# Ordering a mixture's experts by token count on the chip: places of 128 and of 64 tokens take turns in the expert stage

## The chip, the cores and the metric

One core of a Trainium2 chip runs the whole program once; the metric is the device time of that one launch in microseconds (us). TensorE (PE) multiplies, VectorE (DVE) and ScalarE (ACT) work elementwise, GpSimd (POOL) makes masks and constants, SyncE (SP) issues nearly all loads, and 16 DMA engines carry them.

## The reference, cut to what matters

Two residual layers over x, 256 tokens of 1024 channels, float32. Layer 0 is attention beside a short convolution, then a dense SwiGLU; layer 1 is a recurrent block, then a mixture of 8 experts, each token going to two. The mixture is what the change touches:

```
logits = xf @ w_router                      # [256, 8]
top_logits, top_idx = lax.top_k(logits, 2)
gates = softmax(top_logits)
for each expert e, for its tokens xb:
    hb = silu(xb @ w_gate[e]) * (xb @ w_up[e])   # 1024 -> 3584
    yb = hb @ w_down[e]                          # 3584 -> 1024
out[token] += gate * yb
```

On the inputs that are timed, the reference's router gives the experts 0 to 7, in this order, 67, 78, 65, 56, 63, 63, 62 and 58 tokens.

## The kernel before, in words

All weights are float32 and are read once, from one array laid out in the order of use, in loads of 128 x 2048 elements (1 MB) into a ring of tiles. SP issues them in order; each waits until the ring's tile is free. Each half of a load, a *piece* of 128 x 1024, is split into a high and a low part of fewer bits: ScalarE copies the high part (`hl_of`, L242), VectorE subtracts it from the piece (L243). TensorE then makes three products for every pair of a stationary and a moving tile (`mm3`, L221 to 224): high by high, high by low, low by high.

The expert stage (`experts`, L845) takes the experts 0 to 7 in turn, 128 tokens each. For every expert the hidden width is cut into 7 blocks f of 512. A block has 12 pieces: four each of the gate and the up projection (`g`, `u`) and four of the down projection (`d`) of the block before. The tokens are the stationary side, [channel, 128 tokens]; the weights move through, 512 columns at a time. So a piece is 2 x 3 products of 512 columns, whatever the number of tokens that the expert really has.

What surrounds the products:

- `choices` (L786) ranks every token within its expert. `choose` (L899) makes a 0/1 matrix [token, slot] for two experts at a time, and `gather` (L906) multiplies the normed tokens by it, both parts, in products of 256 columns (two experts of 128 slots).
- After the gate's last piece ScalarE takes its SiLU from PSUM (L998); after the up projection's, VectorE multiplies (L1002). Two pieces later (`TURN`), `turn` (L959) transposes the hidden block on TensorE (four transposes, L962) and splits it (L242, L243).
- `factors` and `back` prepare norm factors and the way back; `out_parts` and `combine` (L967, L976) bring an expert's rows back into the residual in products of 256 columns.
- `gates` (L820) comes at the down projection of block 3, and counts the fullest expert. If an expert has more than 128 tokens, a second pass over all experts runs (L1060 to 1063).

Order of the work: the stage is written out by hand (`manual_schedule`, L1024). After the products of piece n come what they set off (`follow`, L992), what is due at n (`at`), and then the splits of pieces up to n + 5 (`AHEAD`, the number of tile pairs for split pieces; L1055). Each engine works through its own instructions in this order. The ring has 9 tiles, and 2 more from the earlier layers' buffers; in the first round 2 halves besides (`source`, L871).

```
for n in range(len(pieces)):
    products(n)
    ...
    follow(n)
    for fn, a in later.pop(n, ()):
        fn(*a)
    while ready < min(n + 1 + (AHEAD if n < len(pieces) - END else ENDA), ...):
        prepare(ready)
        ready += 1
```

Of the kernel before, what the change touches and what calls it, by code (L numbers as in the profile page):

```python
# [9 lines left out]
F32 = mybir.dt.float32  # L10
# [15 lines left out]
NE = 8  # L26
# [17 lines left out]
# Products that keep the tensor engine's clock up: at the start, and on both sides of the ranks.  # L44
# [13 lines left out]
TURN = 2  # L58
# The ring with the tiles that the first rounds of the experts' weights use besides.
# [16 lines left out]
def _chunks():  # L76
    """The weights in the order in which they are used: name and elements per partition."""
# [12 lines left out]
    prev = []  # L90
    for e in range(NE):
        for f in range(NF):
            c += [(f"m{m}{e}_{f}_{i}", 2048) for m in "gu" for i in range(2)]
            c += prev
            prev = [(f"md{e}_{f}_{i}", 2048) for i in range(2)]
    return c + prev
# [8 lines left out]
NW = _o  # L105


def body(ctx, tc, x_d, w_d, prm_d, bv_d, rt_d, out_d):
# [8 lines left out]
    t2 = ctx.enter_context(tc.tile_pool(name="t2", bufs=5))  # L117
# [33 lines left out]
    def warm(n):  # L151
        """Keeps the clock of the tensor engine up where it would else wait long."""
        p = pz()
        for _ in range(n):
            T.matmul(p[:, 0:P], onesb, onesb, start=True, stop=True)

    def weave(chain, filler):
        """Emits a step of the one, a step of the other, and so on."""
        live = [chain, filler]
        while live:  # L160
            for g in list(live):
                if next(g, live) is live:
                    live.remove(g)
# [4 lines left out]
    # ---- inputs and constants  # L168
# [33 lines left out]
    def halves(k):  # L202
        """A load into two of the tiles of half the size."""
# [22 lines left out]
    def rsqrt(ss, n, inv):  # L226
        """(ss * inv + eps) ** -0.5 by Newton's steps."""
# [12 lines left out]
    def hl_of(src, oh, ol):  # L240
        """src as the sum of two parts of fewer bits."""
# [3 lines left out]
    def scaled(gk):  # L245
        """The residual by the norm's gain, in two parts; the norm's other factor comes later."""
# [9 lines left out]
    def norm_factor(spread=True):  # L256
        """1 / rms of every token: one a partition [128, 2], and along the free dimension [128, 256]."""
# [44 lines left out]
            # Two sums share a bank: only the bank's first product clears it.  # L302
# [31 lines left out]
    def wide_steps(src, hT, o, n):  # L334
        """o[:, j, :] (two of them in a bank) = columns j of the load, [n / 128, 8, 128], by hT."""
# [12 lines left out]
    # ---- layer 0: attention and short convolution  # L348
# [7 lines left out]
    # The distance, and where there is none to be seen, a number that the softmax doesn't survive.  # L356
# [31 lines left out]
    def attention():  # L388
# [36 lines left out]
        # The first block's eight heads see one block of keys, the second's, four at a time, two.  # L425
# [113 lines left out]
    # -8 * softplus(-lambda), its logarithm as a series in t / (2 + t).  # L539
# [20 lines left out]
    # ---- layer 0: SwiGLU  # L560
# [27 lines left out]
    # ---- layer 1: recurrent block  # L588
# [566 lines left out]
```

## Time and profile before

| | |
|---|---|
| time, median of 3 runs | 1446.46 us (1446.17 to 1446.46) |
| span of the profiled execution, first to last instruction | 1447.3 us |
| busy in it: PE, DVE, ACT, POOL | 98%, 83%, 71%, 0% |
| read from HBM | 424.77 MB, 294 GB/s over the span |
| loads of the expert stage | 336 of 1 MB |

The profiled execution is one of its own, beside the timed runs; its span is its time, 0.8 us above their median. The stages, from the stretches of the profile: layer 0 and the recurrent block until about 450 us, the experts from there to the end. A busy engine in these views is one that has an instruction under way; matmuls overlap, so the start-to-start distance of equal instructions is the better price.

### The profile page before, as it was taken

How to read it: one execution, taken by the hardware profiler on the slowest of the kernel's cores; microseconds unless marked ns; L12 is line 12 of the kernel's file. 1: busy time of each engine (PE TensorE's matmuls, PEld its weight loads, DVE VectorE, ACT ScalarE, POOL GpSimd, SP SyncE). 2: the span in 40 equal slices, each digit the busy share in tenths (PEclk: the TensorE clock that was granted, in tenths of full speed). 3: DMA queues.
4: the chain of work that ended last, by engine and by line, in shares of the span. 5: the costliest groups of instructions: out<-in, count | busy, mean ns of one | idle time of the engine just before them, and what ended most of it. 6: DMA issues, size and time to landing. Idle time of an engine off the chain costs nothing.

```text
span 1447.3 us, 20977 instructions
## 1 busy us (share of the span) xinstructions
PE 1422.2 (98%) x8083; PEld 1241.0 (86%) x8083; DVE 1198.5 (83%) x1365; ACT 1025.4 (71%) x1195; POOL 3.0 (0%) x15
## 2 busy tenths in 40 slices
PE   8999999999999999999999999999999999999997
PEld 7799999999988888888888888888888888888886
DVE  6667555556887999988999998899999889999986
ACT  6445444444796888788788778878887887887874
POOL 0000000000000000000000000000000000000000
PEclk9999999999999999999999999999999999999999
DMA  9434455553447899999999989999999999999980
GB/s 374 181 118 174 175 185 194 175 177 144 175 146 287 316 350 383 347 351 360 342 374 375 367 339 365 352 344 377 374 359 351 352 353 348 376 376 343 377 318 32
DMA packets 61451, 427.25 MB, mean 295 GB/s; under 512 B 7200, under 2 KB 7200, under 8 KB 11296
## 3 DMA queue, kind: packets, MB, share of 16 engines
q1 hardware_dynamic: 60624, 425.22, 77.5%
q8 instruction: 65, 1.06, 0.3%
q10 hardware_dynamic: 720, 0.62, 0.1%
q14 instruction: 42, 0.34, 0.1%
HBM read 424.77 MB, written 1.05 MB: 294 GB/s over the span
## 4 chain that ended last, share of the span: by engine, by line
PE 85%; DVE 6%; ACT 4%; DMA 3%; issue 1%; SPq 0%; ACTq 0%
PE pw L222 17%; PE pw L223 17%; PE pw L224 17%; PE pa L222 7%; PE pa L224 7%; PE pa L223 7%; DVE L L243 4%; PE pa L304 3%; PE pa L303 3%; PE pa L305 3%; DMA w<-in_w_dram 2%; PE pz L962 1%; ACT H L217 1%; PE pz L913 1%; ACT H L242 1%
## 5 line engine op out<-in xcount | busy, mean ns | idle before, releaser
L243 DVE TENSOR_TENSOR L<-w,H 128x1024 fp32r<-128x1024 f32 x545 | 647.1, 1218 | 70.0 <-ACT H L242 50.3
L242 ACT ACTIVATE H<-w 128x1024 fp32r<-128x1024 f32 x545 | 563.6, 1056 | 90.7 <-PE pw L224 56.5
L222 PE MATMUL pw<-H,b 128*128 128x512 f32 x896 | 350.3, 391 | 0.7 <-ACT b L914 0.7
L223 PE MATMUL pw<-L,b 128*128 128x512 f32 x896 | 349.1, 390 | 0.0
L224 PE MATMUL pw<-H,b 128*128 128x512 f32 x896 | 348.8, 389 | 0.0
L217 ACT ACTIVATE H<-w 128x1024 fp32r<-128x1024 f32 (+1 forms) x138 | 143.1, 1046 | 169.4 <-PE pw L223 101.5
L218 DVE TENSOR_TENSOR L<-w,H 128x1024 fp32r<-128x1024 f32 (+1 forms) x138 | 165.8, 1207 | 92.2 <-ACT H L217 92.1
L224 PEld LDWEIGHTS pw<-H,b 128*128 128x128 f32 x896 | 168.2, 188 | 35.9 <-ACT b L914 0.6
L222 PEld LDWEIGHTS pw<-H,b 128*128 128x128 f32 x896 | 168.4, 188 | 34.5 <-ACT b L914 1.4
L223 PEld LDWEIGHTS pw<-L,b 128*128 128x128 f32 x896 | 168.4, 188 | 33.0
L222 PE MATMUL pa<-H,b 128*128 128x512 f32 x480 | 192.1, 402 | 4.3 <-ACT H L217 4.3
L222 PE MATMUL pw<-b,H 128*128 128x256 f32 x672 | 191.4, 285 | 2.7 <-DVE b L608 1.4
L224 PE MATMUL pw<-b,L 128*128 128x256 f32 x672 | 191.2, 284 | 0.1
L223 PE MATMUL pw<-b,H 128*128 128x256 f32 x672 | 190.9, 285 | 0.0
L224 PE MATMUL pa<-H,b 128*128 128x512 f32 x480 | 186.9, 389 | 0.0
L223 PE MATMUL pa<-L,b 128*128 128x512 f32 x480 | 186.8, 389 | 0.0
L243 DVE TENSOR_TENSOR L<-b,H 128x1024 fp32r<-128x1024 f32 x128 | 152.8, 1220 | 17.8 <-ACT H L242 14.1
L242 ACT ACTIVATE H<-b 128x1024 fp32r<-128x1024 f32 x128 | 132.7, 1057 | 18.7 <-PE pw L224 11.1
L222 PEld LDWEIGHTS pw<-b,H 128*128 128x128 f32 x672 | 129.4, 193 | 3.8 <-issue 3.7
L224 PEld LDWEIGHTS pw<-b,L 128*128 128x128 f32 x672 | 129.5, 193 | 0.3 <-DVE L L218 0.3
L223 PEld LDWEIGHTS pw<-b,H 128*128 128x128 f32 x672 | 129.4, 193 | 0.2
L222 PEld LDWEIGHTS pa<-H,b 128*128 128x128 f32 x480 | 90.8, 190 | 20.6 <-ACT H L217 4.5
(209 smaller groups left out, 1456.7 us busy)
## 6 DMA issues: line engine op xcount, KB each, us to landing
w<-in_w_dram SPq DMA_DIRECT2D x331, 1024.0 KB, 5.1
b<-in_w_dram SPq DMA_DIRECT2D x60, 1024.0 KB, 5.1
w<-in_w_dram SPq DMA_DIRECT2D x12, 512.0 KB, 6.8
b<-in_w_dram SPq DMA_DIRECT2D x8, 512.0 KB, 6.7
w<-in_w_dram SPq DMA_DIRECT2D x4, 768.0 KB, 7.9
x_sb<-in_x_dram SPq DMA_DIRECT2D x4, 256.0 KB, 7.6
out_dram<-x_sb SPq DMA_DIRECT2D x2, 256.0 KB, 3.1
out_dram<-x_sb ACTq DMA_DIRECT2D x2, 256.0 KB, 3.1
```

The lines of the kernel that those rows point to most:

```text
L217: A.activation(h[:, :n], src, AF.Copy)
L218: V.tensor_sub(l[:, :n], src, h[:, :n].bitcast(F32))
L222: T.matmul(o, a[0], b[0], start=first, stop=False)
L223: T.matmul(o, a[0], b[1], start=False, stop=False)
L224: T.matmul(o, a[1], b[0], start=False, stop=last)
L242: A.activation(oh, src, AF.Copy)
L243: V.tensor_sub(ol, src, oh.bitcast(F32))
L303: T.matmul(o, h[:, c], m[0][:, ks[i], :], start=f and d % 2 == 0, stop=False, skip_group_check=True)
L304: T.matmul(o, h[:, c], m[1][:, ks[i], :], start=False, stop=False, skip_group_check=True)
L305: T.matmul(o, l[:, c], m[0][:, ks[i], :], start=False, stop=z and d % 2 == 1, skip_group_check=True)
L913: T.matmul(p[:, k * S:(k + 1) * S], src[:, t, d:d + P], sel[q][t], start=t == 0, stop=t == 1)
L962: T.transpose(p[:, k * P:(k + 1) * P], sg[:, k * P:(k + 1) * P], ident)
```

## The change

Experts no longer run in the order of their number. After the choices the kernel counts the tokens of every expert and orders the experts by count on the chip; expert 0 always comes first in the order, so that its weights can be loaded before the order is known. Places 0, 2, 4, 6 (`HEAVY`) hold 128 tokens and take the first four experts of the order, places 1, 3, 5, 7 (`LIGHT`) hold 64 tokens and take the others. A light place's stationary tile holds 64 tokens' high part beside their low part, so a product by the weight's high part and one by its low part do all (`mm`): 2 x 2 products a piece. Three blocks of place 0 come first (`LEAD`), then light and heavy blocks take turns, and light blocks are left at the end.

The loads of places 1 to 7 take their address from a register that SP reads from the order (`fetch`). In a light block ScalarE copies gate and up projection out of PSUM, and eight full-precision products by two stacked identities of 64 (`ii`) transpose them and add the two parts; SiLU, multiplication and split come after that, on 64 columns a chunk. `turn` moves from 2 to 5 pieces after the up projection; `gates` moves to the first down projection. Ring tiles go from 9 to 8; small tiles go from 5 to 8 (`b2`) and from 6 to 8 (`b1`). The weights' layout in memory puts each expert's weights together. A second pass over all experts runs if a place has more tokens than it holds.

```diff
-N_RING = 9
+N_RING = 8
-N_B1 = 6
+N_B2 = 8
+N_B1 = 8
-TURN = 2
+TURN = 5
...
+HEAVY = (0, 2, 4, 6)
+LIGHT = (1, 3, 5, 7)
+UNITS = ((0,), (1, 3), (2,), (4,), (5, 7), (6,))
+LEAD = 3
...
+    def places():
+        p = pz()
+        for t in R2:
+            T.matmul(p[:, 0:8], onesb, mask[:, t, :], start=t == 0, stop=t == 1)
+        key, pos, need = sv()[:, 0:8], sv()[:, 0:8], sv()[:, 0:8]
+        V.scalar_tensor_tensor(key, p[:, 0:8], float(NE), tie, OP.mult, OP.add)
+        sq = [P, NE, NE]
+        V.tensor_tensor(oh, key[:, None, :].to_broadcast(sq), key[:, :, None].to_broadcast(sq), OP.is_gt)
+        V.tensor_reduce(pos, oh, AX.X, OP.add)
...
+        V.tensor_scalar(cnt, cm[:, 0:1], 0.0, None, OP.max)
...
+        V.tensor_copy(perm, pf)
+        placed(rankp, rank)
...
+            a = [(p, f) for p in HEAVY for f in range(NF)]
+            b = [(p, f) for p in LIGHT for f in range(NF)]
+            order = a[:LEAD]
+            a = a[LEAD:]
+            while a or b:
+                order += b[:1] + a[:1]
+                a, b = a[1:], b[1:]
...
+        def fetch(m, p, f, i, w=None, cuts=1):
+            if rest or p == 0:
+                return load(f"m{m}{p}_{f}_{i}", w, cuts)
+            if p not in regs:
+                regs[p] = nc.values_load(perm[0:1, p:p + 1], engines=[mybir.EngineType.SP], min_val=1, max_val=NE - 1,
...
+            src = w_exp[bass.ds(regs[p], 1), o:o + 2048 * P].rearrange("e (p n) -> (e p) n", p=P)
...
+                nc.sync.dma_start(w[:, c:c + k], src[:, c:c + k])
+            return w
...
+        def gather(u, b):
...
+            o = o.rearrange("p (e j a s) -> p e j a s", e=len(ps), j=2, a=2)
+            for j in R2:
+                d = (2 * b + j) * P
+                for a in R2:
+                    for t in R2:
+                        T.matmul(o[:, :, j, a, :], (xh3, xl3)[a][:, t, d:d + P], sel[u][:, t, :, 0:64],
+                                 start=t == 0, stop=t == 1)
...
+        def mm(o, a, h, l, first, last):
+
+            if isinstance(a, tuple):
+                mm3(o, a, (h, l), first, last)
+            else:
+                T.matmul(o, a, h, start=first, stop=False)
+                T.matmul(o, a, l, start=False, stop=last)
...
+        def turn_light(p, f, g, u):
+
+            o = pz()
+            for j, src in enumerate((g, u)):
+                for k in range(4):
+                    c = j * S + k * 64
+                    T.matmul(o[:, c:c + 64], src[:, k * P:(k + 1) * P], ii, start=True, stop=True)
+            s = b2()
+            A.activation(s[:, 0:S], o[:, 0:S], AF.Silu)
+            V.tensor_mul(s[:, S:], o[:, S:], s[:, 0:S])
+            hid[p, f] = s
+
+        def split_light(p, f):
+            h = b2(F32R)
+            v = h.rearrange("p (k a s) -> p k a s", k=4, a=2)
+            hl_of(hid[p, f][:, S:].rearrange("p (k s) -> p k s", k=4), v[:, :, 0, :], v[:, :, 1, :])
+            hid[p, f] = h
...
+                if p in heavy:
+                    V.tensor_mul(sg, psum["u"], sg)
+                    at(n + (1 if last else TURN), turn, p, f, sg)
+                else:
+                    u = b2()
+                    A.activation(u, psum["u"], AF.Copy)
+                    at(n + (1 if last else TURN), turn_light, p, f, sg, u)
+                    at(n + (3 if last else TURN + 4), split_light, p, f)
...
+        if not rest:
+            at(1, places)
+            at(pn(1, "d", 0), gates)
...
-    experts(0)
-    # Tokens beyond an expert's first 128.
+    experts(False)
+
     most = nc.values_load(cnt[0:1, 0:1], min_val=0, max_val=S)
-    with tc.If(most > P):
-        experts(P)
+    with tc.If(most > 0):
+        experts(True)
```

## Rows read from the trace of the kernel before

**Rows 1.** The page, part 1: busy us (share of the span) xinstructions.

```profile
PE 1422.2 (98%) x8083; PEld 1241.0 (86%) x8083; DVE 1198.5 (83%) x1365; ACT 1025.4 (71%) x1195; POOL 3.0 (0%) x15
```

**Rows 2.** The page, part 4: the chain that ended last, by engine.

```profile
PE 85%; DVE 6%; ACT 4%; DMA 3%; issue 1%; SPq 0%; ACTq 0%
```

**Rows 3.** Stretches: length, then each engine's busy us; columns in the first line.

```profile
core 0: us, PE busy (x) PEld busy (x) DVE busy (x) ACT busy (x) POOL busy (x), PEclk, DMA share, GB/s
14.00:34.00 20.00, 20.00 (x133) 18.30 (x132) 16.84 (x43) 12.21 (x18) 0.00 (x0) 1.00 1.02 424
...
470.00:1425.00 955.00, 953.95 (x4417) 790.20 (x4417) 868.46 (x835) 763.86 (x819) 0.00 (x0) 1.00 0.92 351
600.00:1400.00 800.00, 799.10 (x3705) 662.27 (x3705) 725.42 (x688) 638.59 (x684) 0.00 (x0) 1.00 0.94 359
```

**Rows 4.** Waits of the load queue, 600 to 1400 us: total us, times, longest.

```profile
SPq L199 <- DVE L L243: 686.7, 273, 4.0
```

**Rows 5.** Groups by form, 600 to 1400 us: count, busy us, mean ns, idle before.

```profile
L243 DVE TENSOR_TENSOR L<-w,H 128x1024 fp32r<-128x1024 f32 x448 | 533.7, 1221 | 61.0 <-ACT H L242 43.6 <-PE pz L924 3.5 <-DMA w<-in_w_dram 1.4
...
L998 ACT ACTIVATE b<-pw,gs 128x512 f32<-128x512 f32 x45 | 31.1, 690 | 14.8 <-PE pw L224 14.8
...
L902 DVE TENSOR_TENSOR b<-iota,rank 128x256 fp32r<-128x256 f32 x6 | 2.3, 418 | 0.0
```

**Rows 6.** Timeline of PE around a hidden block's transposes: start us, us, what.

```profile
1010.53 0.40 PE L223 MATMUL pa<-L,b 128*128 128x512 f32 x1
1010.76 0.39 PE L224 MATMUL pa<-H,b 128*128 128x512 f32 x1
1010.99 0.60 PE L962 MATMUL pz<-ident,b 128*128 128x128 f32 x4
1011.35 0.48 PE L222 MATMUL pa<-H,b 128*128 128x512 f32 x1
1011.66 0.39 PE L223 MATMUL pa<-L,b 128*128 128x512 f32 x1
```

**Rows 7.** Timeline of DVE, 904 to 910 us.

```profile
904.30 2.35 DVE L243 TENSOR_TENSOR L<-b,H 128x1024 fp32r<-128x1024 f32 x2
906.57 0.68 DVE L243 TENSOR_TENSOR b<-pz,b 128x512 fp32r<-128x512 f32 x1
907.17 2.35 DVE L243 TENSOR_TENSOR L<-b,H 128x1024 fp32r<-128x1024 f32 x2
```

**Rows 8.** Timeline of ACT, 901 to 903 us.

```profile
901.47 1.05 ACT L242 ACTIVATE H<-w 128x1024 fp32r<-128x1024 f32 x1
902.42 1.05 ACT L242 ACTIVATE H<-b 128x1024 fp32r<-128x1024 f32 x1
```

**Rows 9.** Timeline of PE in attention, 80 to 85 us: start us, us, what.

```profile
80.30 0.28 PE L223 MATMUL pw<-b,H 128*128 128x256 f32 x1
80.42 0.28 PE L224 MATMUL pw<-b,L 128*128 128x256 f32 x1
...
82.62 0.66 PE L481 MATMUL pz<-b,b 128*128 128x64 f32 x4
83.09 0.36 PE L224 MATMUL pw<-b,L 128*128 128x256 f32 x1
...
83.41 1.45 PE L481 MATMUL pz<-b,b 128*128 128x64 f32 x12
84.66 0.36 PE L223 MATMUL pw<-b,H 128*128 128x256 f32 x1
```

**Rows 10.** Timeline of DVE: the norm's chain, first and last of 13.

```profile
457.73 0.16 DVE L230 TENSOR_SCALAR s<-pz 128x2 f32<-128x2 f32 x1 [2.24 <-PE pz L813]
...
459.90 0.16 DVE L237 SCALAR_TENSOR_TENSOR s<-s,s 128x2 f32<-128x2 f32 x1
```

**Rows 11.** Load issues, 14 to 34 and 600 to 1400 us: count, size, us to landing.

```profile
w<-in_w_dram SPq DMA_DIRECT2D x5, 1024.0 KB, 9.8
...
w<-in_w_dram SPq DMA_DIRECT2D x221, 1024.0 KB, 5.2
```

More of the change, by code (lines that the diff above doesn't have):

```diff
@@ L868, in experts @@
         later = {}
-        xg, fac, pts, psum, hid, ys, yp = {}, {}, {}, {}, {}, {}, {}
+        regs = {}
+        sel, xg, fac, pts, psum, hid, ys, yp = {}, {}, {}, {}, {}, {}, {}, {}
+        def fetch(m, p, f, i, w=None, cuts=1):
[3 more added lines that the diff above has]
+                regs[p] = nc.values_load(perm[0:1, p:p + 1], engines=[mybir.EngineType.SP], min_val=1, max_val=NE - 1,
+                                         skip_runtime_bounds_check_because="a sum over a row with a single one")
+            if w is None:
+                w = ring.tile([P, 2048], F32, tag="w", name=nm("w"))
+            o = OFF[f"m{m}0_{f}_{i}"][0] - OFF["mg0_0_0"][0]
+            src = w_exp[bass.ds(regs[p], 1), o:o + 2048 * P].rearrange("e (p n) -> (e p) n", p=P)
+            k = 2048 // cuts
+            for c in range(0, 2048, k):
+                nc.sync.dma_start(w[:, c:c + k], src[:, c:c + k])
+            return w
         def source(n):
-            m, e, f, i = pieces[n]
+            m, p, f, i = pieces[n]
             if i % 2 == 0:
-                k = f"m{m}{e}_{f}_{i // 2}"
                 c = n // 2 - 2
-                if not base and n < 4:
+                if not rest and n < 4:
                     held[0] = early[n // 2]
-                elif not base and c < TURNS4 * ROUNDS and c % TURNS4 >= TURNS4 - 2:
-                    held[0] = halves(k)
+                elif not rest and c < TURNS4 * ROUNDS and c % TURNS4 >= TURNS4 - 2:
+                    held[0] = halves(f"m{m}{p}_{f}_{i // 2}")
                 else:
-                    if not base and c < TURNS4 * ROUNDS:
+                    if not rest and c < TURNS4 * ROUNDS:
                         c = c % TURNS4
@@ new lines, in sel_of @@
+        def sel_of(p, t):
+            u = unit_of[p]
+            return sel[u][:, t, units[u].index(p), :]
+        def gather(u, b):
+            ps = units[u]
+            o = (pa if ps[0] == 0 and not rest else pz)()
+            if ps[0] in heavy:
+                a, b = b // 2, b % 2
+                for j in range(4):
+                    d = (4 * b + j) * P
+                    for t in R2:
+                        T.matmul(o[:, j * P:(j + 1) * P], (xh3, xl3)[a][:, t, d:d + P], sel_of(ps[0], t),
+                                 start=t == 0, stop=t == 1)
+                A.activation(xg[ps[0]][a][:, b * 512:(b + 1) * 512], o, AF.Copy)
+                return
+            o = o.rearrange("p (e j a s) -> p e j a s", e=len(ps), j=2, a=2)
+            for j in R2:
+                d = (2 * b + j) * P
+                for a in R2:
+                    for t in R2:
+                        T.matmul(o[:, :, j, a, :], (xh3, xl3)[a][:, t, d:d + P], sel[u][:, t, :, 0:64],
+                                 start=t == 0, stop=t == 1)
+            for e, p in enumerate(ps):
+                A.activation(xg[p][:, b * 256:(b + 1) * 256], o[:, e, :, :, :].rearrange("p j a s -> p (j a s)"), AF.Copy)
@@ new lines, in factors, with back @@
+        def factors(p, cols):
+            o = pz()
+            sc = scl if rest or p == 0 else sclp
+            for t in R2:
+                T.matmul(o[:, cols], sel_of(p, t).bitcast(F32), sc[:, t, p, cols], start=t == 0, stop=t == 1)
+            if p not in fac:
+                fac[p] = sm.tile([P, 2], F32, tag="gs", name=nm("gs"), bufs=6)
+            V.tensor_copy(fac[p][:, cols], o[:, cols])
+        def back(p):
+            o = pz()
+            for t in R2:
+                T.transpose(o[:, t * P:(t + 1) * P], sel_of(p, t).bitcast(F32), ident)
+            pt = b1(F32R)
+            A.activation(pt, o[:, 0:S], AF.Copy)
+            pts[p] = pt
@@ L1026, in experts @@
                 prepare(n)
-            if not base:
+            if not rest:
                 router(3)
@@ L1033, in experts @@
             choose(0)
-            if not base:
+            if not rest:
                 squares(3)
@@ L1037, in experts @@
                 prepare(n)
-            for a in R2:
-                gather(0, 0, a)
-            if not base:
+            for b in (0, 2):
+                gather(0, b)
+            if not rest:
                 low()
@@ L1044, in experts @@
                 products(n)
-                if n < 3:
-                    for a in R2:
-                        gather(0, n + 1, a)
-                if n == 0 and not base:
+                if n == 1:
+                    for b in (1, 3):
+                        gather(0, b)
+                if n == 0 and not rest:
                     norm()
```

216 lines of the change are left out of this document (116 added, 100 removed).

## The prediction

> **What bounds the kernel now.** I read the page first, then the stretches, then the waits, then single instructions. TensorE is busy for 98% of the span [rows 1] and makes 85% of the chain that ended last [rows 2]. The change lies in the expert blocks, from about 452 us to the end, so the stretch view decides. In 600 to 1400 us TensorE is busy for 799.1 of 800 us at a granted clock of 1.00 (2.4 GHz), VectorE for 725, ScalarE for 639, and the DMA engines show a share of 0.94 while they move 359 GB/s [rows 3]. A busy TensorE need not be the bound, so I asked who waits: the load queue sat 686.7 us waiting for VectorE to free a place in the ring [rows 4]. The loads are therefore ahead, and TensorE sets the pace. Its single instructions agree: a product of 512 columns starts every 0.227 us [rows 6], so a piece of six takes 1.36 us. VectorE's split of a piece takes 1.135 us from start to start (904.30 to 906.57 us for two) [rows 7]; the 1.22 us of the group [rows 5] overlaps its neighbour. ScalarE's half of a split takes 0.95 us (901.47 to 902.42) [rows 8].
>
> So per block of 12 pieces (gate, up and the down projection before): TensorE 12 x 1.36 + 0.44 for the four transposes = 16.8 us; VectorE 12 x 1.135 + 2 x 0.60 (906.57 to 907.17 [rows 7]) = 14.8 us; 6.29 MB of weights. The margin beside TensorE is only 2 us. That is the reason why the saving can't be taken whole.
>
> **The change part by part.** (a) A light expert's stationary tile holds 64 tokens' high part beside their low part, so four products per piece do what six did. Four of eight experts, 7 blocks each, are 28 light blocks; 28 x 12 pieces x 2 products = 672 products fewer, at 0.227 us: -152.5 us, all of it on TensorE, which bounds.
>
> (b) The light hidden block no longer goes through four transposes, 0.44 us with what follows them (1010.99 us to the products back in step at 1011.66, less 0.227) [rows 6]. It goes through eight full-precision products of 64 columns, which also add the two parts. The same form is in attention: the eight calls of its last group at L481 leave 4 + 12 instructions, which hold TensorE from 82.62 to 83.09 and from 83.41 to 84.66 us [rows 9], so 0.104 to 0.118 us each. I take 0.11: two instructions a call make 16 x 0.11 = 1.76 us a block, and 28 x (1.76 - 0.44) = +37 us.
>
> (c) Gathers: 128 products of 256 columns become 128 of 128 columns (four heavy places) and 64 of 2 x 64 columns (two light pairs). A 256-column product starts every 0.12 us (80.30, 80.42) [rows 9]. 64 more at 0.115 are +7 us; were the narrow ones as slow as a 512-column product, 192 x 0.227 - 128 x 0.115 = +29. I take 7, as 0.115 is the narrow row nearest to it; below nothing is excluded by the higher count.
>
> (d) Placing experts: about 14 dependent small VectorE operations after the second piece, and 4 more with the gates. The norm's chain has 12 steps from 457.73 to 459.90 us, 0.18 each [rows 10]. Its 2.6 to 3.3 us stand in the stretch where few pieces are ready, so +3; the bounds are 0 (hidden by the splits ahead) and 6. Only ScalarE's and VectorE's queues are held by it. SP reads the place's expert number before the first light load, the 17th of the stage; by then the chain is long done, and the seven reads (one a place) stand in a queue that waits anyway [rows 4]. Register addresses for the loads: no row shows them. An issue can grow to the load's period, 800 us / 273 = 2.9 us, before it counts; I take 0 and make the rest a rival. The gates' two sigmoids and their VectorE steps come two blocks earlier, with the same count; the later turn (5 pieces instead of 2) has 12 pieces until its result is used, so it delays nothing: both 0.
>
> (e) VectorE: a light block has one 256-column multiply and one split of 256 columns, 0.42 us each at most [rows 5], in place of two of 0.60. With one heavy and one light block as a pair: TensorE 16.8 + 12 x 0.907 + 1.76 + 0.1 = 29.5 us; VectorE 24 x 1.135 + 1.2 + 0.8 = 29.2; ScalarE 24 x 0.95 and six more copies and SiLUs at 0.69 or less [rows 5], 26.9 at most. TensorE stays the bound by 1%, with five split pieces (5.7 us of VectorE) as cushion against the 1.6 us by which a light half outruns VectorE.
>
> (f) DMA: a pair is 12.58 MB. At 14 to 34 us the DMA engines carry 424 GB/s at a share of 1.02 [rows 3]: 29.7 us, 0.2 more than TensorE. At 359 / 0.94 = 382 GB/s it would be 32.9. Which of the two is the ceiling? In the early stretch loads land 9.8 us after issue, in the expert stage 5.2 [rows 11], with 1.05 MB asked for every 2.9 us; so the early queue is about twice as deep. When DMA becomes the bound the ring of 10 empties and the queue gets deep, which is the early state. I take 424: 28 x 0.2 = +5 us; at 382, 335 MB after 470 us (351 GB/s x 955) [rows 3] end at 1347, and with about 15 to 25 us for the last loads' products the kernel ends at 1362 to 1372. The gathers, combines and the start, some 50 us in which no weights are consumed (452 to 1441 us less 56 blocks of 16.8), let the loads catch up in both cases.
>
> By the Trainium skill, "DMA: Bandwidth & Descriptors", section "Where 436 GB/s comes from", loads from HBM are bound at about 358 GB/s per core, which would leave this change nothing. The row of 424 GB/s disagrees [rows 3]; the Trainium skill's "HBM Reference", section "Specifications (TRN2)", has about 425 GB/s for a core that streams alone, with which that row agrees.
>
> (g) The last three blocks are light, at 14.3 us for VectorE and 14.8 for DMA (6.29 MB at 424) against 12.75 for TensorE: 2 us late each beyond the cushion, +4. The chain after the last products (scaling, two products, the add) is unchanged. One ring place fewer in the earlier layers: the queue there waits for places with TensorE full, 0 to 2 us; taken as 0.
>
> Sum: -152.5 + 37 + 7 + 3 + 5 + 4 = -96.5. From the span of 1447.3 us that is 1350.8. That is the profiled execution's own time from first to last instruction; the median of the timed runs, 1446.46, is 0.8 us below it, so 1350 to 1351 by the runs. I forecast **1351 us**.
>
> **The rivals.** First, DMA is already the ceiling: 359 GB/s and a share of 0.94 are all there is. Then 335 MB from 470 us on last until 1404, and the end is 1419 to 1447, so from 2% faster down to nothing; the page named above gives this. For it: the share of 0.94. Against it: the 686.7 us wait of the load queue and the 424 GB/s. Chance 0.08, of which 0.02 within 0.2%.
>
> Second, the engines don't overlap as the sums do. VectorE follows ScalarE's SiLU, which follows the 1.76 us of narrow products, in order, in a queue that has 1% to spare. If each light block costs VectorE a wait of 1.76 + 0.35 us that nothing makes up, 28 x 2.1 = 59 us are added: 1410; half of it is 1380. For it: VectorE and TensorE within 0.3 us a pair. Against: the turn comes five pieces after the up projection, and five pieces lie ready. Chance 0.14.
>
> Third, on the slower side: the second pass over all experts. It runs when a place has more tokens than it holds. The counts on these inputs, from the reference's router, are 78, 67, 65, 63, 63, 62, 58 and 56; the fullest light place holds 63 of 64. Two tokens chosen otherwise on the chip decide, and the price is another stage of 336 loads, 830 us at 424 GB/s: about 2200 us. Against it: the router's products are in full precision, and a token changes its experts only at a near tie. Chance 0.04. With it I count register-addressed loads that cost SP over 2.9 us each, which would slow the stage from that point on at 336 us per microsecond: 0.03, 1500 us or more.
>
> **How the numbers follow.** The forecast case has 0.71: 1329 to 1372. Its low end leaves out (d), (f) and (g) (-12) and the gathers (-7) and takes 0.104 for the narrow products (-3), so 1329; its high end is DMA at 382. The range takes in the second rival up to two thirds of its price: 1329 to 1396, some 0.82 of the chances. Faster by over 0.2% (about 3 us, what a measurement of this kernel can tell from no change): 0.71 + 0.14 + 0.06 = 0.91. Within: 0.02. Slower: 0.07.
>
> **What would show it.** Right: about 672 fewer 512-column products; a steady pair of blocks of 29.5 to 31 us; DMA at 400 GB/s or more with landing times above 5.2 us; VectorE busy beyond its 725 of 800; TensorE with short idle times before light products, ended by VectorE's split. The narrow products appear as 448 instructions at 0.11 us. Wrong: DMA that stays near 360 GB/s while the load queue no longer waits for VectorE (first rival); idle time of VectorE ended by ScalarE's SiLU or by the narrow products (second); loads after the last block (third). If TensorE is idle and all others too, the order of the queues is what I have missed.

## The result and the profile after

The changed kernel takes **1391.28 us** (median of 4 runs, 1387.46 to 1392.17), the kernel before 1446.32 beside it: a ratio of 0.961, 95% interval 0.960 to 0.963. That is 55 us faster. The forecast of 1351 is missed by 40 us, though the time lies in the range (1329 to 1396). So the question is where 40 us of a gain of 96 went.

The profiled execution spans 1390.4 us. Its page, part 1 and the chain by engine, to be read against [rows 1, 2]:

```profile
PE 1342.5 (97%) x7811; PEld 1157.8 (83%) x7811; DVE 1171.6 (84%) x1379; ACT 1010.9 (73%) x1251; POOL 4.2 (0%) x29
...
PE 67%; DVE 18%; issue 9%; ACT 5%; DMA 1%; DVEq 0%; SPq 0%; ACTq 0%
```

TensorE lost 80 us of busy time, and VectorE's share of the chain rose from 6% to 18%: the set of engines on the path has changed. Stretches of the changed kernel, columns as in [rows 3]; the second is one pair of blocks without gathers or combines:

```profile
460.00:470.00 10.00, 9.26 (x52) 7.36 (x51) 9.31 (x31) 4.04 (x5) 0.00 (x0) 1.00 0.17 43
560.00:590.00 30.00, 29.57 (x136) 23.61 (x135) 28.59 (x28) 26.26 (x30) 0.00 (x0) 1.00 1.01 414
600.00:1300.00 700.00, 681.60 (x3242) 553.46 (x3241) 654.98 (x644) 584.96 (x678) 0.00 (x0) 1.00 0.97 384
```

Before, TensorE was idle for 0.9 of 800 us [rows 3]; now it is idle for 18.4 of 700. VectorE is idle for 45 of 700, so it isn't full either. The DMA engines move 384 GB/s, so 359 was no ceiling. TensorE, VectorE and the DMA engines are near full and none is full: that is the picture of engines that wait for one another. The waits in 600 to 1300 us (total us, times, longest):

```profile
ACT b L1093 <- PE pz L1091: 43.1, 21, 2.5
DVE L L250 <- ACT H L249: 33.2, 56, 1.3
PEld pw L1053 <- DVE L L250: 23.5, 46, 0.9
ACT H L249 <- PE pw L231: 19.2, 60, 0.8
PEld pz L1118 <- DVE b L1110: 10.9, 6, 2.0
PE pz L1118 <- DVE b L1110: 9.7, 6, 1.8
```

Read them as a ring. ScalarE's half of a split (L249) waits for TensorE to be done with a tile, VectorE's half (L250) for ScalarE's, and TensorE's product of a low part (L1053) for VectorE's. (A wait of PEld and one of PE with the same releaser are one wait seen twice.) The last two lines are a second place: the combine. TensorE's timeline shows both, and the period of a pair (the first and the third line):

```profile
559.58 1.89 PE L1091 MATMUL pz<-ii,b 128*128 128x64 f32 x16
...
580.36 0.50 PE L1053 MATMUL pw<-L,b 128*128 128x512 f32 x1 [0.43 <-DVE L L250]
...
590.47 1.89 PE L1091 MATMUL pz<-ii,b 128*128 128x64 f32 x16
...
736.99 0.38 PE L1117 MATMUL pz<-b,b 128*128 128x256 f32 x1
739.13 0.39 PE L1118 MATMUL pz<-b,b 128*128 128x256 f32 x1 [1.76 <-DVE b L1110]
```

From one group of 16 narrow products to the next it is 30.9 us, where the prediction had 29.5 for TensorE. In the combine the second product stands 2.1 us behind the first. VectorE over the same pair and the same combine:

```profile
562.87 3.75 DVE L250 TENSOR_TENSOR L<-w,H 128x1024 fp32r<-128x1024 f32 x3 [0.52 <-ACT H L249]
567.33 1.23 DVE L250 TENSOR_TENSOR L<-w,H 128x1024 fp32r<-128x1024 f32 x1 [0.71 <-ACT H L249]
...
579.09 12.56 DVE L250 TENSOR_TENSOR L<-w,H 128x1024 fp32r<-128x1024 f32 x11
...
736.07 2.35 DVE L250 TENSOR_TENSOR L<-b,H 128x1024 fp32r<-128x1024 f32 x2
738.33 0.74 DVE L1110 SCALAR_TENSOR_TENSOR b<-pa,gs,b 128x512 fp32r<-128x512 f32 x1
```

In the heavy half VectorE stands idle for 0.52 and 0.71 us; in the light half it runs eleven splits back to back and TensorE waits. Both happen in one pair: the cushion (the tiles of split pieces that lie ready for TensorE) is full, then empty. Later, at the combine, VectorE works off two splits before it comes to the scaled rows (L1110) that TensorE already waits for.

Last the load queue. In 600 to 1300 us and in 380 to 500 us, the lines that matter:

```profile
SPq L954 <- DVE L L250: 540.5, 249, 6.4
...
SPq L1210 <- DVE tmp L874: 18.0, 1, 18.0
```

The first answers to [rows 4]: the queue still waits for ring places most of the time. The second is new: the register read of the overflow count (L1210), which belongs to the test after the last expert, stands in the load queue ahead of the experts' loads and held them for 18 us; the row of 460 to 470 us above shows 43 GB/s.

### The profile page after: what moved, and what is told of

Its sections match the earlier page's. It is cut to its first block, busy times and chain, and to the rows that moved or that the text cites. A ratio compares the mean times of both kernels' runs of the same rounds, so it can differ in the third digit from the quotient of the medians.

```text
span 1390.4 us, 21184 instructions
## 1 busy us (share of the span) xinstructions
PE 1342.5 (97%) x7811; PEld 1157.8 (83%) x7811; DVE 1171.6 (84%) x1379; ACT 1010.9 (73%) x1251; POOL 4.2 (0%) x29
## 4 chain that ended last, share of the span: by engine, by line
PE 67%; DVE 18%; issue 9%; ACT 5%; DMA 1%; DVEq 0%; SPq 0%; ACTq 0%
DVE L L250 14%; PE pw L229 10%; PE pw L230 10%; PE pw L231 9%; PE pw L1053 4%; PE pa L230 4%; PE pa L229 4%; PE pa L231 4%; PE pz L1091 3%; PE pa L310 3%; PE pa L312 3%; PE pa L311 3%; PE pw L1052 3%; ACT H L249 2%; ACT H L224 1%
## 5 line engine op out<-in xcount | busy, mean ns | idle before, releaser
L250 DVE TENSOR_TENSOR L<-w,H 128x1024 fp32r<-128x1024 f32 (+1 forms) x533 | 620.9, 1215 | 39.2 <-ACT H L249 35.6
L249 ACT ACTIVATE H<-w 128x1024 fp32r<-128x1024 f32 (+1 forms) x533 | 537.6, 1053 | 35.7 <-PE pw L231 17.0
L224 ACT ACTIVATE H<-w 128x1024 fp32r<-128x1024 f32 (+1 forms) x138 | 143.1, 1045 | 170.6 <-PE pw L230 101.6
L225 DVE TENSOR_TENSOR L<-w,H 128x1024 fp32r<-128x1024 f32 (+1 forms) x138 | 165.9, 1208 | 93.6 <-ACT H L224 93.5
L1053 PE MATMUL pw<-L,b 128*128 128x512 f32 x448 | 182.3, 407 | 7.5 <-DVE L L250 7.5
L229 PE MATMUL pw<-H,b 128*128 128x512 f32 x448 | 178.4, 398 | 0.0
L1052 PE MATMUL pw<-H,b 128*128 128x512 f32 x448 | 178.3, 398 | 0.0
L230 PE MATMUL pw<-L,b 128*128 128x512 f32 x448 | 175.0, 391 | 1.4 <-DVE L L250 1.4
L231 PE MATMUL pw<-H,b 128*128 128x512 f32 x448 | 174.9, 390 | 0.2 <-ACT b L1015 0.2
L250 DVE TENSOR_TENSOR L<-b,H 128x1024 fp32r<-128x1024 f32 x140 | 164.5, 1217 | 8.4 <-ACT H L249 7.9
L249 ACT ACTIVATE H<-b 128x1024 fp32r<-128x1024 f32 x140 | 141.8, 1055 | 9.7 <-PE pw L231 5.3
L1053 PEld LDWEIGHTS pw<-L,b 128*128 128x128 f32 x448 | 84.1, 188 | 46.4 <-DVE L L250 31.9
L229 PE MATMUL pa<-H,b 128*128 128x512 f32 (+1 forms) x256 | 99.8, 392 | 4.1 <-ACT H L224 4.1
L310 PE MATMUL pa<-b,H 128*128 128x256 f32 x352 | 99.7, 286 | 3.0 <-ACT b L249 3.0
L230 PE MATMUL pa<-L,b 128*128 128x512 f32 (+1 forms) x256 | 102.1, 399 | 0.0
L231 PE MATMUL pa<-H,b 128*128 128x512 f32 (+1 forms) x256 | 100.0, 390 | 0.0
```

The source lines that it names most:

```text
L224: A.activation(h[:, :n], src, AF.Copy)
L225: V.tensor_sub(l[:, :n], src, h[:, :n].bitcast(F32))
L229: T.matmul(o, a[0], b[0], start=first, stop=False)
L230: T.matmul(o, a[0], b[1], start=False, stop=False)
L231: T.matmul(o, a[1], b[0], start=False, stop=last)
L249: A.activation(oh, src, AF.Copy)
```

## Experiments

Each was timed four times, and each group ran beside the kernel before, whose medians in the four groups were 1450.9, 1451.5, 1448.7 and 1447.0 us. Between groups the ratios are therefore the safer comparison. The change itself spreads over 4.7 us from run to run, so differences of 2 or 3 us are not read.

The last column is the expert part of the profiled execution alone: from the first product that ranks the tokens (L806 in the change) to the last instruction. In the kernel before it is 995.6 us (451.67 to 1447.3). In the change and in the three edits of it that do next to nothing it lies between 935.4 and 936.8 us, so it tells small effects apart better than the whole time.

| run | us | ratio to before (95%) | expert part, us |
|---|---|---|---|
| the change | 1391.3 | 0.961 (0.960 to 0.963) | 936.8 |
| third product put back | 1499.0 | 1.034 (1.030 to 1.037) | 1042.7 |
| SiLU later | 1388.3 | 0.958 (0.954 to 0.961) | 935.9 |
| six pieces ahead | 1378.5 | 0.951 (0.949 to 0.953) | 915.7 |
| narrow products early | 1383.9 | 0.955 (0.952 to 0.957) | 928.7 |
| not alternating | 1394.2 | 0.962 (0.961 to 0.964) | 943.4 |
| not alternating, six ahead | 1402.8 | 0.969 (0.966 to 0.971) | 942.1 |
| combine two pieces later | 1381.7 | 0.952 (0.950 to 0.955) | 930.5 |
| its second half later | 1390.3 | 0.959 (0.957 to 0.962) | 935.4 |
| six ahead, second half later | 1375.1 | 0.948 (0.946 to 0.951) | 914.3 |
| **six ahead, combine behind** | **1361.0** | **0.940 (0.938 to 0.942)** | **900.3** |
| the same, narrow products early | 1365.9 | 0.942 (0.940 to 0.945) | 903.6 |
| count later | 1389.0 | 0.957 (0.955 to 0.960) | 935.4 |

### What the products are worth

```diff
                 T.matmul(o, a, h, start=first, stop=False)
-                T.matmul(o, a, l, start=False, stop=last)
+                T.matmul(o, a, l, start=False, stop=False)
+                T.matmul(o, a, h, start=False, stop=last)
```

> Each step of a light piece multiplies by the high part a second time: three products, as in a heavy piece, so the 672 products are put back and all else of the change stays (its output holds the high part twice in the light places). Theory (the terms of the sum are right and only the coupling of the queues was left out): TensorE sets the pace again, a pair takes 16.3 + 16.3 + 1.7 + 0.4 = 34.8 us, and the 35 to 40 us of waits for splits go; 1391 + 152.5 less those: 1500 to 1510. Rival (the narrow products or gathers cost more than the terms say, and the splits wait for other reasons): nothing is absorbed, 1535 to 1545.

Measured: 1499.0. The period of a pair on TensorE's timeline:

```profile
567.47 1.89 PE L1092 MATMUL pz<-ii,b 128*128 128x64 f32 x16
...
602.41 1.89 PE L1092 MATMUL pz<-ii,b 128*128 128x64 f32 x16
```

34.9 us against 34.8 expected. So with TensorE as the bound the sum of its products holds. In the change the 672 products are worth 106 us (1042.7 - 936.8 in the expert part; 105 by the ratios), not 152.5: some 47 us of their saving are lost because TensorE no longer sets the pace alone.

### ScalarE's wait, or the cushion

Two readings of the ring of waits: ScalarE is held by its SiLU behind the narrow products (the rival of the prediction), or the five tiles of split pieces are too few.

```diff
+            hid[p, f] = o
+
+        def gate_light(p, f):
+            o = hid[p, f]
             s = b2()
             A.activation(s[:, 0:S], o[:, 0:S], AF.Silu)
...
                     at(n + (1 if last else TURN), turn_light, p, f, sg, u)
+                    at(n + (2 if last else TURN + 2), gate_light, p, f)
```

> In light blocks ScalarE's SiLU and VectorE's multiply stand two pieces behind the narrow products instead of right behind them, so ScalarE's wait of 2 us per block is gone from its queue. Theory in its first form (ScalarE's wait for the narrow products delays the splits): about 1 us per pair of blocks, 20 to 30 us less, 1361 to 1371. Theory in its second form (while TensorE does narrow products it frees no split buffer, so the engines behind stand still whatever ScalarE waits for; only a deeper cushion helps): 0 to 8 us less. Rival (VectorE is saturated): nothing.

Measured: 1388.3, 3 us less and within the spread (1 us less in the expert part). The first form fails; the second (0 to 8 us) and a saturated VectorE (nothing) can't be told apart by this run. The waits of that kernel in 600 to 1300 us:

```profile
ACT H L249 <- PE pw L231: 58.7, 79, 2.6
```

In the change that line had 19.2 us, and the SiLU's had 43.1. The SiLU's line is gone, and ScalarE stands in front of the next split instead, since no tile is free. Its longest wait, 2.6 us, is the narrow products seen from there. Next, the cushion itself:

```diff
-N_RING = 8
-N_HL = 5
+N_RING = 7
+N_HL = 6
```

> Six pieces split ahead in place of five, one place fewer in the ring of loads (7). Theory in its second form (the cushion is too shallow for the swing between a heavy half, where VectorE outruns TensorE, and a light half, where it falls behind): 1.0 of the 1.4 us that a pair loses come back, 20 to 30 us less, 1361 to 1371. Theory in its first form: 0 to 8 us less. Rival (VectorE saturated): nothing, 1391. Rival (DMA the bound): nothing or a few us more, as the ring is shorter.

Measured: 1378.5. The sign is the theory's; 13 us (15 by the ratios) are less than the 20 to 30 expected. The period of a pair on TensorE's timeline, and one of the waits in 600 to 1300 us:

```profile
562.66 1.89 PE L1091 MATMUL pz<-ii,b 128*128 128x64 f32 x16
...
592.46 1.78 PE L1091 MATMUL pz<-ii,b 128*128 128x64 f32 x15
```

```profile
PEld pw L1053 <- DVE L L250: 2.6, 15, 0.2
```

The pair falls from 30.9 to 29.8 us: 1.1 of the 1.4 us lost, as expected, and TensorE's waits for splits go from 23.5 to 2.6 us. VectorE does the same work in both kernels, so it was not saturated at 30.9. The expert part gains 21 us (936.8 to 915.7), within the 20 to 30. The whole gains less because the edit, which paid for the sixth tile with a place of the ring, costs something ahead of the experts. The first ranking product in the change and here:

```profile
453.56 0.17 PE L806 MATMUL pz<-mask,tri 128*128 128x8 bf16 x1
...
458.23 0.18 PE L806 MATMUL pz<-mask,tri 128*128 128x8 bf16 x1 [0.41 <-DVE mask L803]
```

In the five kernels with six tiles and seven places it stands at 458.2 to 462.2 us, in the change and its seven variants with five and eight at 449.2 to 454.1. So the layers ahead of the experts are 4 us or more slower in every kernel with this edit. The shorter ring is the likely half of it; six tiles with eight places were not run.

The place of the narrow products:

```diff
-                    at(n + (1 if last else TURN), turn_light, p, f, sg, u)
+                    at(n + (1 if last else 2), turn_light, p, f, sg, u)
```

> The narrow products of a light block come two pieces after its up projection, in place of five: near the end of the light run of pieces, where the cushion is empty, and not inside the heavy run, where it is full. Five pieces of depth, as in the change. Theory (the cushion swings by more than it holds; TensorE's 1.7 us of narrow products are of use to the splits only where the cushion is empty): a pair of 30.9 us becomes 29.9 or so, 15 to 25 us less over the kernel, 1366 to 1376. Rival (where TensorE stands does not matter, since VectorE's work of 29.2 us and its hand-overs fill the pair): nothing. Rival (ScalarE's copy of the up projection comes too late for products two pieces on): 5 to 20 us more.

Measured: 1383.9, but not for the reason given. The free pair is as long as before:

```profile
555.62 1.56 PE L1091 MATMUL pz<-ii,b 128*128 128x64 f32 x13
...
586.50 1.67 PE L1091 MATMUL pz<-ii,b 128*128 128x64 f32 x14
```

30.9 us: where TensorE stands still does not matter to the cushion. That part of the theory fell. What the traces show of the 7 us lies at the combines: TensorE's waits for the scaled rows went from 9.7 to 4.7 us (L1118 on L1110, 600 to 1300 us).

The use of alternation is to carry VectorE's lead from a heavy half into a light one. The order alone undone:

```diff
-LEAD = 3
+LEAD = 28
```

> The change with its order alone undone: the blocks of the four heavy places first, then those of the four light ones. Theory (a light block by itself is set by VectorE, 14.3 us, or the loads, 14.9 us at 422 GB/s, and can't use what a heavy one leaves over; a pair that alternates takes 30.9): a pair costs 16.8 + 14.9 to 15.5 = 31.7 to 32.3 us, 25 pairs, 20 to 35 us more than the change, 1411 to 1426. Rival (VectorE's work sets the average in either order): 1388 to 1394.

Measured: 1394.2, 3 us above the change (7 in the expert part). My theory missed and the rival's number came, though not by the rival's reason. TensorE's timeline, two heavy blocks and two light ones, and the stretch of light blocks:

```profile
631.15 0.60 PE L1080 MATMUL pz<-ident,b 128*128 128x128 f32 x4
...
647.96 0.60 PE L1080 MATMUL pz<-ident,b 128*128 128x128 f32 x4
...
1014.03 1.89 PE L1091 MATMUL pz<-ii,b 128*128 128x64 f32 x16
...
1028.33 1.89 PE L1091 MATMUL pz<-ii,b 128*128 128x64 f32 x16
```

```profile
1000.00:1100.00 100.00, 94.27 (x444) 72.25 (x444) 98.51 (x101) 87.89 (x109) 0.00 (x0) 0.98 1.01 418
```

A heavy block alone takes 16.8 us (TensorE's time), a light one alone 14.3 (VectorE's: busy for 98.5 of 100 us; the DMA engines are full too, but no engine waits for a load in 520 to 1350 us). Their sum is 31.1, and the alternating pair takes 30.9. With five tiles alternation is worth 0.2 us a pair: hardly any of the lead is carried over. If the cushion is the reason, which I thought of only after this result, alternation should be worth more with six tiles. The fourth case, not alternating with six tiles:

```diff
-LEAD = 3
+LEAD = 28
-N_RING = 8
-N_HL = 5
+N_RING = 7
+N_HL = 6
```

> Heavy places first, light ones after, with six pieces split ahead and seven ring places: the fourth of four cases (alternating or not, five or six pieces). Theory (depth is worth something only because it carries VectorE's lead from a heavy half into a light half): without alternation the sixth piece brings nothing; blocks of 16.6 and 14.3 us as in the run with five, and 0 to 5 us more for the shorter ring: 1392 to 1400. Rival (a sixth piece speeds the hand-overs by itself, alternating or not): as much less as in the alternating kernel, 1378 to 1384.

Measured: 1402.8, 9 us more than with five. The light block still takes 14.3 us, and TensorE waits elsewhere:

```profile
1009.02 1.89 PE L1091 MATMUL pz<-ii,b 128*128 128x64 f32 x16
...
1018.60 0.50 PE L1052 MATMUL pa<-H,b 128*128 128x512 f32 x1 [1.27 <-DVE b L250]
...
1023.28 1.89 PE L1091 MATMUL pz<-ii,b 128*128 128x64 f32 x16
```

In 950 to 1350 us the waits for low parts (L1053) fall from 29.8 to 1.0 us, and those for the hidden block's split (L1052 on b L250) rise from 16.7 to 30.5: VectorE fills the light block either way. The 9 us do not lie in the expert part at all. The first ranking product, in order, with five tiles and with six:

```profile
449.15 0.18 PE L806 MATMUL pz<-mask,tri 128*128 128x8 bf16 x1 [0.41 <-DVE mask L803]
...
459.22 0.18 PE L806 MATMUL pz<-mask,tri 128*128 128x8 bf16 x1 [0.41 <-DVE mask L803]
```

It comes 10 us later with six tiles and the shorter ring (449.15 is the earliest of the kernels with eight places, 459.22 the middle one of those with seven). In the expert part the four cases are 936.8 and 915.7 us alternating (five and six tiles), 943.4 and 942.1 in order. A sixth tile is worth 21 us with alternation and 1 without; faster hand-overs would show in both orders, a saturated VectorE in neither. That fits the theory, and the first form and the saturated VectorE both fail. It is not a test of every other reason, since in order the blocks already stand at TensorE's sum and at VectorE's and leave a sixth tile little to win.

### The combine

An expert's rows are scaled by ScalarE and VectorE (L1109, L1110), and TensorE multiplies them (L1117, L1118) from one piece later on.

```diff
-                    at(n + 1 + j, combine, p, i - 1 + j)
+                    at(n + 3 + j, combine, p, i - 1 + j)
```

> An expert's products that bring its rows back go two pieces later. Theory: TensorE's waits before them for the scaled rows (18.9 us in all, 6 before the change) go, 8 to 13 us less, 1378 to 1383. Rival (VectorE's or the DMA's total work sets the end, so that a wait taken from TensorE comes back elsewhere): 0 to 3 us less.

Measured: 1381.7, as the theory had it (6 us less in the expert part). But its trace shows a new wait in three of the combines. TensorE's timeline has one:

```profile
740.57 0.41 PE L1117 MATMUL pz<-b,b 128*128 128x256 f32 x1 [3.12 <-DVE b L250]
```

VectorE's timeline at that place, and then two stretches, during the wait and after it:

```profile
738.70 1.21 DVE L250 TENSOR_TENSOR L<-w,H 128x1024 fp32r<-128x1024 f32 x1
739.83 0.68 DVE L250 TENSOR_TENSOR b<-pz,b 128x512 fp32r<-128x512 f32 x1
```

```profile
736.00:740.50 4.50, 1.45 (x9) 0.94 (x7) 4.50 (x6) 3.50 (x5) 0.00 (x0) 1.00 1.01 410
740.50:744.00 3.50, 3.43 (x13) 3.05 (x14) 3.47 (x5) 1.06 (x1) 0.00 (x0) 0.54 0.88 311
```

Two tiles of PSUM (pz) serve the combine and the transposes. The combine's second quarter needs the tile that the transposes hold until VectorE has split them (739.83), and that split stands behind others. I took from this that the second half was what had to move, and left the first:

```diff
-                    at(n + 1 + j, combine, p, i - 1 + j)
+                    at(n + i // 2 * 2 + 1 + j, combine, p, i - 1 + j)
```

> Only the second half of an expert's combine goes two pieces later, the first stays. Theory: both the wait of 2 us for the scaled rows (seven times) and the wait of 3 us that the later first half met in the run before it (its PSUM tile is held by the hidden block's split) are gone: 12 to 16 us less than the change, 1375 to 1379. Rival (a wait taken away at the combines comes back at the next splits): as with both halves late, 1381 or more.

Measured: 1390.3, a miss. The wait of 2 us sits at the first half, as it did in the change:

```profile
733.36 0.38 PE L1117 MATMUL pz<-b,b 128*128 128x256 f32 x1
735.50 0.39 PE L1118 MATMUL pz<-b,b 128*128 128x256 f32 x1 [1.77 <-DVE b L1110]
```

With six tiles the same edit does as little beyond the depth itself:

```diff
-N_RING = 8
-N_HL = 5
+N_RING = 7
+N_HL = 6
...
-                    at(n + 1 + j, combine, p, i - 1 + j)
+                    at(n + i // 2 * 2 + 1 + j, combine, p, i - 1 + j)
```

> Six pieces split ahead, seven ring places, and the second half of the combine two pieces later. Theory (two separate losses): 1378.5 less 12 to 15, so 1363 to 1367. Rival (with pairs at 29.8 us the loads at 422 GB/s are now the bound, so what TensorE no longer waits at the combines it waits for loads): 1374 to 1379, and waits of ScalarE for loads.

Measured: 1375.1, 3 us below six tiles alone. Neither the two losses added up nor did the loads stand in the way: the waits list of 520 to 1350 us has no wait for a load. The edit was aimed at the wrong half. So the rule was taken from the queue instead of from one trace: what VectorE is handed after piece n stands behind the splits of the pieces ahead, so TensorE can count on it only as many pieces later.

```diff
-N_RING = 8
-N_HL = 5
+N_RING = 7
+N_HL = 6
...
-                    at(n + 1 + j, combine, p, i - 1 + j)
+                    at(n + AHEAD + 1 + 2 * j + 2 * (i // 2), combine, p, i - 1 + j)
```

> Six pieces split ahead, seven ring places, and each combine is put behind the pieces that stand in VectorE's queue ahead of its input: the four quarters seven to thirteen pieces after their down piece, two pieces apart. Theory (the scaled rows wait behind six splits, so a combine needs to wait as many pieces, and two PSUM tiles serve the four quarters, so these need room between them): the waits of 1.4 to 2.0 us at the second product of a combine, 14 us in all, are gone, without new ones at its first product: 1360 to 1366. Rival (VectorE's 29.2 us of 29.8 in a pair are the bound, so the time lost at combines is VectorE's own extra work there): nothing, 1373 to 1379.

Measured: **1361.0**, 17 us below six tiles alone (16 by the ratios, 15 in the expert part). Its stretches, then its waits in 600 to 1300 us (the two lines of L1118 are gone, the largest at a combine is the second line here), then the largest of its load queue:

```profile
600.00:1300.00 700.00, 698.55 (x3389) 578.66 (x3388) 678.09 (x673) 607.17 (x708) 0.00 (x0) 1.00 1.00 403
560.00:590.00 30.00, 30.00 (x143) 24.77 (x142) 29.45 (x29) 26.62 (x32) 0.00 (x0) 1.00 1.01 422
```

```profile
ACT b L1093 <- PE pz L1091: 41.9, 22, 2.0
...
PEld pz L1117 <- DVE x_sb L1120: 2.1, 3, 0.7
```

```profile
SPq L954 <- DVE L L250: 447.5, 220, 3.8
```

TensorE is busy for 698.6 of 700 us again. ScalarE still waits 41.9 us for narrow products (L1093), as in the change, and with TensorE full it costs nothing. Together with the run that took this wait away for 3 us, it shows that this line was not what the change lost its time to. This version beats both kernels, by 2% and by 6%. On top of it the early narrow products:

```diff
-                    at(n + (1 if last else TURN), turn_light, p, f, sg, u)
+                    at(n + (1 if last else 2), turn_light, p, f, sg, u)
```

> The run before, and the narrow products two pieces after the up projection. Theory (an early turn helped only because it left the combines' place): with the combines out of the way it brings nothing more, within 3 us of the run before. Rival (the place of the narrow products in the heavy run costs by itself): 4 to 8 us less than the run before.

Measured: 1365.9, 5 us more. The gain of 7 us without depth is not had a second time, as the theory said. The loss is a little beyond its 3 us; in the two traces 3 us of it lie ahead of the ranking product (462.2 against 459.0 us), where the edit changes nothing, and 3 us in the expert part. There, three waits of the narrow products for a combine's PSUM tile (3.5 us, L1091 on L1120, 600 to 1300 us) are new.

### The read in the load queue

```diff
...
-        V.max(cm, need)
-        V.tensor_scalar(cnt, cm[:, 0:1], 0.0, None, OP.max)
...
+            at(pn(50, "u", 0), fullest)
```

> The overflow count is computed fifty blocks later, so its register read can no longer stand in SP's load queue at 448 us, where it stopped the loads for 18 us. Theory (a queue that holds others in order): the read cost part of the 13 us of TensorE stalls between 450 and 525 us; 3 to 10 us less, 1381 to 1388 us. Rival (loads are the bound of the whole stage): the whole 18 us come back, about 1373. Rival (the cushion of loaded pieces hides the hole): nothing, 1391.

The removed lines stand in `fullest`. Measured: 1389.0, 2 us less, within the spread. Two stretches:

```profile
450.00:460.00 10.00, 9.19 (x91) 8.17 (x90) 7.29 (x20) 8.17 (x12) 0.00 (x0) 1.00 0.94 346
460.00:470.00 10.00, 9.62 (x53) 7.67 (x52) 9.34 (x32) 4.04 (x5) 0.00 (x0) 1.00 0.25 77
```

The read is gone. In 450 to 460 us the loads now move 346 GB/s, where they moved 182 with the read; then they stop all the same, since the ring's places are taken. By 500 us the two kernels have moved nearly as much (256 GB/s over 440 to 500 us without the read, 249 with it), and TensorE was busy for 57.9 of these 60 us in both. So the read's 18 us cost nothing here; the second rival holds.

## Why the prediction was right and where it failed

The time lies in the range, but above the band of the forecast case, which ended at 1372. The range reached up to it by two thirds of the second rival's price, and that rival's mechanism was not the one that acted. So the sign and the larger part of the sum were right, two of its steps failed ((e) and the chains of (g)), and that the range held is in part luck.

**(a) 672 products fewer, (b) narrow products, (c) gathers: right.** TensorE's instructions fall from 8083 to 7811, which is what the parts add up to: 672 fewer, 448 narrow ones for 112 transposes, 64 more in the gathers. The changed trace has a product every 0.227 us, 16 narrow products from 559.58 us to the next product 1.70 us on, where 1.76 was taken, and 16 gather products from 460.59 us in 1.74, 0.109 each where 0.115 was taken. With the products put back the kernel is 47.5 us above the kernel before of its group (1499.0 against 1451.5), 47 in the expert part; (b), (c), (d) and (g) were to give 37 + 7 + 3 + 4 = 51.

**(d) Placing: the price only within that sum, one sentence wrong.** No run measures the 3 us alone. "Only ScalarE's and VectorE's queues are held by it" failed: SP's was held for 18.0 us by a read whose result is needed only at the end of the kernel. The loads ahead hid it.

**(e) is the main step that failed.** "TensorE stays the bound by 1%, with five split pieces (5.7 us of VectorE) as cushion against the 1.6 us by which a light half outruns VectorE." The engine sums are right: 16.8 and 14.3 us are what the blocks take alone, and 29.8 us with six tiles comes close to the 29.5 summed. The cushion was mis-sized. It was counted as five finished pieces; but a tile is taken from the start of ScalarE's half of the split until TensorE's last product of that piece, so several of the five are in work at any time. An estimate from rows: 0.95 us on ScalarE, 1.135 on VectorE and 1.36 on TensorE are 3.4 us for a piece, 2.5 pieces at TensorE's pace, before anything lies finished. Measured, five tiles carried 0.2 us a pair and a sixth 1.1 more, about one split (1.135 us). Why the 2.5 pieces that this estimate leaves did not carry the 1.6 us is open. That TensorE frees no tile during its 1.7 us of narrow products was my guess, and the run that moved them left the pair at 30.9. Deeper than six was not tried: it would cost another ring place.

The second rival had the place nearly right (engines that don't overlap as the sums do; its half price was 1380) and the mechanism wrong: taking ScalarE's wait out of its queue brought 3 us, and leaving it in with six tiles cost nothing.

**(g) "The chain after the last products is unchanged" missed the chains inside.** Each expert but the last ends among other blocks, and its combine hung on VectorE's queue before too: in the trace of before its second product waits 0.16 us, with VectorE well ahead:

```profile
718.07 0.39 PE L982 MATMUL pz<-b,b 128*128 128x256 f32 x1 [0.16 <-DVE b L974]
```

With VectorE behind, TensorE waits there nine times, up to 2.0 us, 13.4 in all (L1118 on L1110, from 455 us on). Moved behind the splits the combine brought 15 to 17 us, somewhat more than these waits; what else is in it was not separated. By the Trainium skill, "PSUM — Partial Sum Buffer", section "Engine vs sequencer instructions", the queues of ScalarE and VectorE are strictly first in, first out; the trace agrees: at 738.33 us the scaled rows come after two splits that TensorE needs later than them. The ring's place that (g) took as 0 did cost nothing to be seen: the first ranking product stands at 451.67 us before and, with eight places, at 449.2 to 454.1. Only the next place, given up for the sixth tile, came with a cost of 4 us or more.

**(f) DMA: the choice of ceiling was right.** 422 GB/s in a free pair at a share of 1.01, landing times up from 5.2 us [rows 11] to 7.3 in the change and 7.9 in the fastest version. There ScalarE waits for no load between 520 and 1350 us, so the loads don't set its 29.8 us; the 5 us of (f), which also count 28 pairs where the order has 25, are not seen. By the Trainium skill, "DMA: Bandwidth & Descriptors", section "Where 436 GB/s comes from", about 358 GB/s a core is the bound; that does not hold here. By the Trainium skill, "HBM Reference", section "Specifications (TRN2)", a core that streams alone has about 425; with that the trace agrees.

Of the 40 us that were missing, 30 came back by the two edits of the fastest version. Its first ranking product:

```profile
458.96 0.17 PE L806 MATMUL pz<-mask,tri 128*128 128x8 bf16 x1
```

Its expert part is 95 us shorter than before (995.6 to 900.3, against the 96.5 summed), and most of the last 10 us lie ahead of it: 458.96 us against 451.67. That the expert part meets the sum so closely is also luck, since free pairs take 29.8 us for 29.5 (up to 7 us in all; their 512-column products start 0.231 us apart on average, not 0.227), while (f) had 5 us for the loads.

## What to carry to other kernels

When an edit takes most of the slack from the bounding engine, its saving is paid out only as far as the buffers between the engines can carry the unevenness: count a buffer as taken from its first writer's start to its last reader's end, and compare what is left with the lead of the long half, not with the mean rates. Whatever an in-order engine is handed behind n prepared pieces is ready n pieces later, so place its reader there. Test a suspected wait by moving it before believing the largest line of a wait list: here the largest (43 us) was harmless, and a line of 11 us was worth 15 to 17. And time an edit by stages: one that takes memory from one buffer for another can gain in one stage (21 us) and pay in another (4 or more).

## What the runs showed that was not expected

A load queue that waits for places is no sign of spare bandwidth: in the fastest version it waits 447.5 of 700 us for one line of VectorE alone, while the DMA engines have a share of 1.00. Its loads land 7.9 us after issue, so the queue can stand still with the engines full. I had read [rows 4] as room; the room was there, but the row didn't show it.

TensorE's clock fell on a short wait. In the kernel with the combine two pieces later, TensorE was busy for 1.45 of the 4.5 us up to 740.5 us, with a wait of 3.12 us; then the granted clock was 0.54 over 740.5 to 744 us (near its lower level, 1.2 GHz), and the products of 256 columns there start 0.21 us apart, where they start 0.12 apart at the upper level. A wait of 3 us thus takes something from what follows as well.
